# The value products of two attention units in one order, and two groups of small transfers issued by GpSimd instead of SyncE

## The chip, the cores and the metric

The kernel runs on one core of a Trainium2 chip. The core has five instruction queues: TensorE (PE, the matmuls, with its weight loads listed as PEld), VectorE (DVE), ScalarE (ACT), GpSimd (POOL) and SyncE (SP). SP issues almost all transfers (DMA); the 16 DMA engines of the core carry them out. The metric is device microseconds of one execution. Of the kernel before, three runs were timed, median 411.48 us (410.52 to 412.81); one more execution was profiled, which took 412.56 us with a span of 410.4 us between its first and last instruction, so 2.2 us lie outside the span.

## The reference

One decoder layer on 512 tokens of width 1024, in float32: two mixers read the same projection, and their outputs are merged and projected.

```
h = x @ w_in + b_in                      # q_a, kv_a, g_nsa, z_a, q_b, f_b, i_b, z_b, gm_a, gm_b
# mixer A: sparse attention, 8 heads in 2 groups, head size 64
o_cmp = softmax(q . kc) @ vc             # kc, vc: keys and values of compressed blocks
o_slc = softmax(q_rope . k_slc) @ v_slc  # blocks chosen; with 512 tokens all 8 blocks are
o_win = softmax(q_rope . k_win) @ v_win  # sliding window of 512
o_a   = g0 * o_cmp + g1 * o_slc + g2 * o_win      # gates: sigmoid(g_nsa), per head
# mixer B: gated linear recurrence in chunks of 64, 4 heads of 128
o_b   = hgrn2(q_b, f_b, i_b)
o_b   = o_b * rsqrt(mean(o_b ** 2) + eps) * norm_g
# merge
y = sigmoid(gm_a) * ((o_a * silu(z_a)) @ w_a) + sigmoid(gm_b) * ((o_b * silu(z_b)) @ w_b)
out = layer_norm(alpha * x + y @ w_out)
```

## The kernel before

**Projections.** Each large product is made of three float32r products (reduced-precision passes over float32 data): the weights and the activations are both split into a high and a low part, and hi·xh, hi·xl and lo·xh are added in PSUM. The weights of the projection come as a stream of tiles of 128 x 1024 (`wraw`, two buffers, one SP transfer each, issued three tiles ahead). For each tile ACT casts the high part (`whi`, L274), DVE subtracts to get the low part (`wlo`, L277; three buffers each), and `proj()` issues 24 products on PE, into one of two `pa` PSUM banks. Weight tile 25 is called `gb1` in the text that follows.

**The order of the work.** `proj()` calls `weave.tick()` once per two k-tiles (six products). Everything else is written as Python generators, started on `_Weave`; each `yield n` says after how many ticks the generator goes on, and the numbers come from the table `D`. So `D` decides where, between the projection's products, each other piece of work is recorded. PE's instructions and the transfers of each issuing queue run in exactly the recorded order (`keep_in_program_order`, in `T.matmul` and in `dma` at L150 and L151). The instructions of DVE and ACT are placed by a scheduler that reads the recorded program, so their order moves when the recorded order moves. Every queue is in order: an instruction that waits holds up all that stand behind it.

**Attention.** The 512 queries are four blocks i of 128; a block attends i + 1 key tiles of 128 in each of two branches (selected, window). The work is in six units, u0 to u5, which are (block 3, branch 0), (3, 1), (2, 0), (2, 1), (1, both), (0, both). `attn_scores` makes the scores in PSUM (`pss`, `pst`, `pso`, two banks each). DVE adds masks (L738), ACT exponentiates (L755), DVE or ACT scales by gate and denominator (L763, L766, L772, L774), and DVE transposes 32 x 32 blocks into the one `big` buffer (L788 to L791). Sixteen SP transfers of 32 rows (L802, shown by the profile with the line of `dma`, L151) then turn `big` into a `turn` buffer, of which there are two.

**The values.** When both units of a block are turned, `values(u)` (L808) multiplies the probabilities by the values: products of 64 x 64 on a quarter of the PE array each. `half` selects the rows 0 to 63 or 64 to 127 of the array, `ab` the columns; each half has a PSUM bank `pso` of its own. For block 3 there are eight tiles, four from each unit. Half 0 goes through the tiles 0 to 7, half 1 begins with tile i + 1, so with the second unit's tiles, and comes to the first unit's afterwards. Each product shows in the trace as two records.

**Mixer B's norm.** `hgrn_norm` transposes and sums the squared outputs of four heads (L512, L513), moves the partial sums between partitions by 16 small transfers (L518), adds them (L521, L522), takes the inverse root on ACT (L525, L526), spreads the result (L533, L534) and multiplies it in (L540, L541). `gates` computes the gates of the attention and moves those of the compressed branch, `gq`, into `gc` by 16 small transfers (L621); `cmp_probs` reads them at L691. Both groups are issued by SP, in the same queue as the weight tiles and the `turn` transfers. POOL only clears a few tiles and makes four small copies (L385).

Of the kernel before, what the change touches and what calls it, by code (L numbers as in the profile page):

```python
# [49 lines left out]
def _columns(name):  # L50

    c = np.arange(_COLS[name], _COLS[name] + 128)
    if name[0] == "q" and name[1] != "b" or name[:2] == "za":
# [16 lines left out]
D = dict(h0=6, h2=6, h3=14, h4=0, h5=7, h6=9, n0=20, n1=4, n2=4, n3=1, n4=3, c0=3, c1=5, c2=2, c3=0, r0=5, p0=2,  # L70
         p1=28, p2=0, s0=7, s2=15, s3=4, e0=4, e1=2, t0=6, t1=11, t2=6, t3=3, a4=8, a5=6, y=2, w0=2, w1=2, x0=0,
         x1=0, e2=2, e3=2, g=3, o0=0, o1=9, o2=9, v=10)
D.update({"x0.za0": 4, "o0.0": 6, "w0.35": 0, "y.o.3": 6, "o1.1": 3, "h2.0": 4, "y.m.6": 8, "w0.33": 5, "w1.10": 4,
# [62 lines left out]
def layer_kernel(ctx: ExitStack, tc: tile.TileContext, xT, xn, w0, wi, wf, wv, small, brow, consts,  # L136
# [13 lines left out]
    def dma(o, i):  # L150
        tc.keep_in_program_order(nc.sync.dma_start(o, i))  # L151
# [37 lines left out]
    def dma_act(o, i):  # L189
        tc.keep_in_program_order(A.dma_start(o, i))  # L190

# [312 lines left out]
    def hgrn_norm():  # L504
# [11 lines left out]
        for a in range(4):  # L516
            for b in range(4):
                dma(parts4[32 * a:32 * a + 32, 64 * b:64 * b + 64], part[32 * b:32 * b + 32])  # L518
            yield 1
# [87 lines left out]
    def gates():  # L607
# [11 lines left out]
        for a in range(4):  # L619
            for m in range(4):  # L620
                dma(gc[32 * m:32 * m + 32, a], gq[32 * a:32 * a + 32, m])  # L621
            yield 2
# [185 lines left out]
    def values(u):  # L808
# [4 lines left out]
        for n in range(len(tiles)):  # L813
            for half in range(2):
                v, st = tiles[(n + half * (i + 1)) % len(tiles)]
                br, j = units[v][1][st // (i + 1)], st % (i + 1)
                late = 2 * (j == i and half != br)
                for ab in range(2):
                    rows, c = slice(64 * half, 64 * half + 64), (128, NV)[br] * br + 64 * ab
                    T.matmul(accs[half][64 * ab:64 * ab + 64, 128 * late:512], vts[j][rows, c:c + 64],  # L820
                             probs[v][rows, st, late:4, 128 * ab:128 * ab + 128],
                             start=n == 0, stop=n == len(tiles) - 1)
# [383 lines left out]
```

## Time and profile before

| | us |
|---|---|
| median of three runs (lowest, highest) | 411.48 (410.52, 412.81) |
| profiled execution | 412.56 |
| its span | 410.4 |
| PE busy in the span | 402.4 (98%) |
| PE weight loads | 325.0 (79%) |
| DVE busy | 294.0 (72%) |
| ACT busy | 213.7 (52%) |
| POOL busy | 5.2 (1%) |

Times in rows of the profile are microseconds from the start of the span. A timeline row gives the start, the duration of a run of equal instructions, the engine, the line, the operation with output and inputs, and in brackets the idle time before it with what ended it. `SPq` is SP's queue as it issues transfers; such a row lasts as long as the issuing did, and the data land later. In the transfers' rows `turn<-big` are the sixteen transfers of a unit, `t<-t` at 32 x 64 the partial sums of mixer B, `gc<-gq` the gates and `wraw` the weight tiles. Engines overlap, so busy shares do not add up. The granted TensorE clock is 1.00 where nothing throttles it.

### The profile page before, as it was taken

What the parts mean: (1) busy time and instruction counts of PE and PEld (TensorE: products, weight loads), DVE (VectorE), ACT (ScalarE), POOL (GpSimd) and SP (SyncE); (2) the same over time, 40 slices, a digit from 0 to 9 for tenths busy, and PEclk for the clock granted to TensorE, in tenths of its full rate; (3) what the DMA queues carried; (4) which work ended last, traced back from release to release, by engine and by line L of the source; (5) the groups of instructions that cost most, each with busy time, mean ns of one, the idle gap of its engine ahead of it and who ended that gap; (6) DMA issues with size and microseconds to landing.
All of it is one profiled execution on the core that took longest, in us unless ns stands there. A gap on an engine that the chain in (4) does not pass through costs nothing.

```text
span 410.4 us, 6085 instructions
## 1 busy us (share of the span) xinstructions
PE 402.4 (98%) x2119; PEld 325.0 (79%) x2119; DVE 294.0 (72%) x675; ACT 213.7 (52%) x442; POOL 5.2 (1%) x17
## 2 busy tenths in 40 slices
PE   9999999999999999999998999999999999999994
PEld 8888888899888887778873878885867888888884
DVE  5906599787665888899999586866432879882773
ACT  3445461643225645786785596981223758458211
POOL 2000000001100000000000000000000000000000
PEclk9999999999999999999998999999999999999999
DMA  7975820143332423471184364364938861053121
GB/s 257 381 237 205 290 79 0 36 150 90 113 94 84 136 79 128 114 196 55 60 212 151 102 176 133 105 204 110 243 99 268 256 198 59 0 168 140 41 112 51
DMA packets 27182, 57.60 MB, mean 140 GB/s; under 512 B 5905, under 2 KB 8337, under 8 KB 27153
## 3 DMA queue, kind: packets, MB, share of 16 engines
q1 hardware_dynamic: 26720, 56.84, 44.5%
q10 hardware_dynamic: 432, 0.39, 0.3%
q8 instruction: 16, 0.26, 0.3%
q14 instruction: 14, 0.11, 0.1%
HBM read 42.12 MB, written 2.10 MB: 108 GB/s over the span
## 4 chain that ended last, share of the span: by engine, by line
PE 84%; DVE 7%; SPq 4%; DMA 2%; issue 1%; ACT 1%; DVEq 0%; ACTq 0%
PE pa L144 53%; PE pss L144 14%; PE pso L144 13%; PE pst L144 4%; SPq L151 4%; DVE t L738 2%; DVE wlo L277 1%; DMA turn<-big 1%; DVE big L788 1%; DVE t L512 1%; DVE t L513 1%; DMA t<-t 0%; ACT t L755 0%; PE pst L148 0%; DVE t L695 0%
## 5 line engine op out<-in xcount | busy, mean ns | idle before, releaser
L144 PE MATMUL pa<-t,whi 128*128 128x512 f32 x640 | 199.8, 393 | 0.0
L144 PEld LDWEIGHTS pa<-t,whi 128*128 128x128 f32 x640 | 118.3, 188 | 29.1 <-issue 4.4
L144 PE MATMUL pa<-t,wlo 128*128 128x512 f32 x320 | 124.7, 390 | 0.0
L277 DVE TENSOR_TENSOR wlo<-wraw,whi 128x1024 fp32r<-128x1024 f32 x44 | 53.6, 1217 | 52.2 <-ACT whi L274 48.8
L274 ACT CAST whi<-wraw 128x1024 fp32r<-128x1024 f32 x44 | 45.9, 1045 | 59.7 <-PE pa L144 50.4
L144 PEld LDWEIGHTS pa<-t,wlo 128*128 128x128 f32 x320 | 60.1, 188 | 12.8
L755 ACT ACTIVATE t<-t,sm_mn 128x512 f32<-128x512 f32 (+3 forms) x64 | 35.2, 553 | 13.3 <-DVE sm_mn L738 13.2
L144 PE MATMUL pso<-t,t 128*128 128x512 f32 (+2 forms) x158 | 33.2, 349 | 0.1
L144 PE MATMUL pss<-t,t 128*128 128x512 f32 (+2 forms) x158 | 30.2, 324 | 0.0
L144 PEld LDWEIGHTS pso<-t,t 128*128 128x128 f32 x158 | 25.8, 198 | 3.9 <-ACT t L233 0.4
L144 PE MATMUL pa<-t,t 128*128 128x512 f32 (+1 forms) x104 | 27.2, 367 | 0.0
L144 PEld LDWEIGHTS pss<-t,t 128*128 128x128 f32 x158 | 23.8, 190 | 2.8
L788 DVE STREAM_TRANSPOSE big<-t 128x512 f32<-128x512 f32 (+3 forms) x48 | 23.4, 523 | 0.4 <-PE pss L144 0.4
L144 PEld LDWEIGHTS pa<-t,t 128*128 128x128 f32 x104 | 18.4, 188 | 3.1
L774 ACT ACTIVATE t<-t,sm_mn 128x128 f32<-128x128 f32 (+3 forms) x39 | 18.0, 522 | 5.0 <-DVE sm_mn L766 4.9
L144 PE MATMUL pso<-turn,t 64*64 64x512 f32 (+1 forms) x160 | 19.1, 599 | 1.4 <-DMA turn<-big 1.4
L144 PE MATMUL pa<-turn,t 128*128 128x512 f32 x64 | 19.9, 389 | 0.0
L144 PE MATMUL pss<-t,whi 128*128 128x512 f32 x64 | 19.7, 389 | 0.0
L201 ACT CAST t<-t 128x512 fp32r<-128x512 f32 x16 | 9.6, 619 | 19.0 <-DVE t L1017 9.8
L144 PEld LDWEIGHTS pso<-turn,t 64*64 64x64 f32 x160 | 6.9, 142 | 13.2 <-issue 11.0
L144 PE MATMUL pst<-t,t 128*128 128x512 f32 (+2 forms) x80 | 15.1, 345 | 0.0
L999 ACT ACTIVATE t<-pa,hbias 128x512 f32<-128x512 f32 x16 | 10.9, 680 | 8.1 <-PE pa L144 8.1
(201 smaller groups left out, 520.9 us busy)
## 6 DMA issues: line engine op xcount, KB each, us to landing
wraw<-in_wf_dram SPq DMA_DIRECT2D x38, 512.0 KB, 3.5
turn<-big SPq DMA_DIRECT2D x48, 128.0 KB, 3.2
wraw<-in_wbr_dram SPq DMA_DIRECT2D x8, 512.0 KB, 4.2
t<-in_wout_dram SPq DMA_DIRECT2D x16, 256.0 KB, 4.5
turn<-big SPq DMA_DIRECT2D x32, 96.0 KB, 2.2
t<-in_wi_dram SPq DMA_DIRECT2D x8, 256.0 KB, 4.8
big<-in_w_dram SPq DMA_DIRECT2D x8, 256.0 KB, 6.4
t<-t SPq DMA_DIRECT2D x32, 64.0 KB, 2.0
```

Of the source, the lines that this page charges most:

```text
L144: return tc.keep_in_program_order(nc.tensor.matmul(*a, **k))
L151: tc.keep_in_program_order(nc.sync.dma_start(o, i))
L201: A.copy(dst_hi, src)
L274: A.copy(hi, raws[i])
L277: V.tensor_tensor(lo, raws[i], hi.bitcast(F32), ALU.subtract)
L512: V.transpose(sqT, osq[h][1])
L513: V.tensor_reduce(part[:, 16 * h:16 * h + 16], sqT.rearrange("p (c d) -> p c d", d=32), AX.X, ALU.add)
L738: V.tensor_tensor_reduce(out=p[:, c], in0=pg[ab][:, 256 * z:][:, c], in1=amask[:, 512 - n:512], op0=ALU.add, op1=ALU.min, scale=-0.125, sc ...
L755: A.activation(p, p, AF.Exp, bias=mn[:, h:h + 1], scale=-1.0, accum_out=den[:, h:h + 1])
L774: A.mul(p, p, d)
L788: V.transpose(to, of)
L999: A.activation(gm[name], ps, AF.Tanh, bias=hbias[:, m:m + 1], scale=0.5)
```

## The change

Three things are changed. First, `values(u)`: for the blocks i of 1 and more both halves go through the first unit's tiles and then the second's. The products are sorted by the columns that their half has done so far; a tile on the diagonal of the other half's branch has 256 columns and not 512, so that the halves come out of step by half a tile. For block 0 half 1 takes the tiles in reverse order, as before. Second, a function `dma_pool` issues transfers from POOL, and the 16 partial-sum transfers of `hgrn_norm` and the 16 transfers of `gates` use it. Third, the table `D` has other delays. Lines move by 1 behind the table, by 4 behind `dma_pool` and by 8 behind `values`: L277 is L281, L521 is L525, L738 is L742, L919 is L927.

```diff
-D = dict(h0=6, h2=6, h3=14, h4=0, h5=7, h6=9, n0=20, n1=4, n2=4, n3=1, n4=3, c0=3, c1=5, c2=2, c3=0, r0=5, p0=2,
+D = dict(h0=6, h2=6, h3=14, h4=0, h5=7, h6=9, n0=20, n1=4, n2=4, n3=0, n4=3, c0=4, c1=5, c2=4, c3=0, r0=5, p0=2,
...
+
+    def dma_pool(o, i):
+        tc.keep_in_program_order(G.dma_start(o, i))
...
         for a in range(4):
             for b in range(4):
-                dma(parts4[32 * a:32 * a + 32, 64 * b:64 * b + 64], part[32 * b:32 * b + 32])
+                dma_pool(parts4[32 * a:32 * a + 32, 64 * b:64 * b + 64], part[32 * b:32 * b + 32])
...
         for a in range(4):
             for m in range(4):
-                dma(gc[32 * m:32 * m + 32, a], gq[32 * a:32 * a + 32, m])
+                dma_pool(gc[32 * m:32 * m + 32, a], gq[32 * a:32 * a + 32, m])
...
         accs = PO(), PO()
-        for n in range(len(tiles)):
-            for half in range(2):
-                v, st = tiles[(n + half * (i + 1)) % len(tiles)]
+        todo = []
+        for half in range(2):
+            at = 0
+            for n, (v, st) in enumerate(tiles if i else tiles[::1 - 2 * half]):
                 br, j = units[v][1][st // (i + 1)], st % (i + 1)
                 late = 2 * (j == i and half != br)
-                for ab in range(2):
-                    rows, c = slice(64 * half, 64 * half + 64), (128, NV)[br] * br + 64 * ab
-                    T.matmul(accs[half][64 * ab:64 * ab + 64, 128 * late:512], vts[j][rows, c:c + 64],
-                             probs[v][rows, st, late:4, 128 * ab:128 * ab + 128],
-                             start=n == 0, stop=n == len(tiles) - 1)
+                todo.append((at, n, half, v, st, br, j, late))
+                at += 4 - late
+        for at, n, half, v, st, br, j, late in sorted(todo):
+            for ab in range(2):
+                rows, c = slice(64 * half, 64 * half + 64), (128, NV)[br] * br + 64 * ab
+                T.matmul(accs[half][64 * ab:64 * ab + 64, 128 * late:512], vts[j][rows, c:c + 64],
+                         probs[v][rows, st, late:4, 128 * ab:128 * ab + 128],
+                         start=n == 0, stop=n == len(tiles) - 1)
```

SP's queue around the transfers of units 0 to 3. Here `turn<-big` of 32 x 1024 are units 0 and 1, of 32 x 768 units 2 and 3; `t_1870` holds the partial sums. Before:

```order
L151 DMA turn<-big 32x1024 x16
L151 DMA wraw<-in_wf_dram 128x1024 x2
L151 DMA t_1870<-t_1870 32x64 x8
L151 DMA wraw<-in_wf_dram 128x1024
L151 DMA t_1870<-t_1870 32x64 x8
L151 DMA wraw<-in_wf_dram 128x1024
L151 DMA turn<-big 32x1024 x16
L151 DMA wraw<-in_wf_dram 128x1024 x5
L151 DMA turn<-big 32x768 x16
L151 DMA wraw<-in_wf_dram 128x1024 x3
L151 DMA turn<-big 32x768 x16
```

And now:

```order
L152 DMA turn<-big 32x1024 x16
L152 DMA wraw<-in_wf_dram 128x1024 x3
L152 DMA turn<-big 32x1024 x16
L152 DMA wraw<-in_wf_dram 128x1024 x6
L152 DMA turn<-big 32x768 x16
L152 DMA wraw<-in_wf_dram 128x1024 x2
L152 DMA turn<-big 32x768 x16
```

The partial sums are gone from between the transfers of units 0 and 1, one weight load has moved behind unit 1's, and one of the three between units 2 and 3 has moved out. On POOL the 16 gate transfers stand behind the four copies of L385 and ahead of two memsets, and the 16 partial-sum transfers are its last work.

PE's queue in the value products of block 3, with buffer numbers: `pso_2294` is half 0's bank and `pso_2295` half 1's; `t2_` are the values. Before (`turn_1874` is unit 0's buffer, `turn_2107` unit 1's):

```order
L144 MATMUL pso_2294<-turn_1874,t2_1019 64x512 x2
L144 MATMUL pso_2295<-turn_2107,t2_1019 64x512 x2
L144 MATMUL pso_2294<-turn_1874,t2_1038 64x512 x2
L144 MATMUL pso_2295<-turn_2107,t2_1038 64x512 x2
L144 MATMUL pso_2294<-turn_1874,t2_1071 64x512 x2
L144 MATMUL pso_2295<-turn_2107,t2_1071 64x512 x2
L144 MATMUL pso_2294<-turn_1874,t2_1137 64x512 x2
L144 MATMUL pso_2295<-turn_2107,t2_1137 64x512 x2
```

And now (`turn_1807` is unit 0's, `turn_2091` unit 1's):

```order
L145 MATMUL pso_2294<-turn_1807,t2_1019 64x512 x2
L145 MATMUL pso_2295<-turn_1807,t2_1019 64x512 x2
L145 MATMUL pso_2294<-turn_1807,t2_1040 64x512 x2
L145 MATMUL pso_2295<-turn_1807,t2_1040 64x512 x2
L145 MATMUL pso_2294<-turn_1807,t2_1071 64x512 x2
L145 MATMUL pso_2295<-turn_1807,t2_1071 64x512 x2
L145 MATMUL pso_2294<-turn_1807,t2_1139 64x512 x2
L145 MATMUL pso_2295<-turn_1807,t2_1139 64x256 x2
L145 MATMUL pso_2295<-turn_2091,t2_1019 64x512 x2
```

The block stands at the same place between the projection's products as before; within it the second unit's buffer is now first touched by the ninth pair of products and not by the second. The block of units 2 and 3 has moved 12 products earlier, that of unit 5 to a later place.

DVE's queue around the eight transposes of units 1 and 2's probabilities (L788 before, L792 now). Before, the subtract of weight tile 25 stood among the masks that read the scores:

```order
L738 ISA t_2225,sm_mn<-pss,t_321 128x384
L738 ISA sm_mn 128x1
L277 TENSOR_TENSOR wlo<-wraw,whi 128x1024
L738 ISA t_2227,sm_mn<-pst,t_321 128x384
L738 ISA sm_mn 128x1
L738 ISA t_2229,sm_mn<-pst,t_321 128x384
```

Now it stands behind the transposes, together with that of tile 26:

```order
L792 STREAM_TRANSPOSE big<-t_2063 128x3x4x32
L792 STREAM_TRANSPOSE big<-t_2065 128x3x4x32
L792 STREAM_TRANSPOSE big<-t_2067 128x3x4x32
L792 STREAM_TRANSPOSE big<-t_2069 128x3x4x32
L281 TENSOR_TENSOR wlo<-wraw,whi 128x1024 x2
L836 TENSOR_TENSOR asum<-asum,pso 128x4x4x32
```

Before, one subtract stood between these transposes and the sum into `asum` (L828, now L836). The cast of tile 25 on ACT (L274, now L278) has likewise moved to the place just ahead of that of tile 26. The sum of the partial sums (L521, now L525) stands earlier than before: one transpose of L699 and the subtract of tile 24 are ahead of it behind the transposes of unit 1, and a transpose, the L927 and a small product come between it and the spreading copies.

More of the change, by code (lines that the diff above doesn't have):

```diff
@@ L67 @@
     0, 128, 256, 260, 772, 1284, 1796, 2308, 2820)
-D = dict(h0=6, h2=6, h3=14, h4=0, h5=7, h6=9, n0=20, n1=4, n2=4, n3=1, n4=3, c0=3, c1=5, c2=2, c3=0, r0=5, p0=2,
-         p1=28, p2=0, s0=7, s2=15, s3=4, e0=4, e1=2, t0=6, t1=11, t2=6, t3=3, a4=8, a5=6, y=2, w0=2, w1=2, x0=0,
-         x1=0, e2=2, e3=2, g=3, o0=0, o1=9, o2=9, v=10)
-D.update({"x0.za0": 4, "o0.0": 6, "w0.35": 0, "y.o.3": 6, "o1.1": 3, "h2.0": 4, "y.m.6": 8, "w0.33": 5, "w1.10": 4,
[23 rows of a table removed]
+D = dict(h0=6, h2=6, h3=14, h4=0, h5=7, h6=9, n0=20, n1=4, n2=4, n3=0, n4=3, c0=4, c1=5, c2=4, c3=0, r0=5, p0=2,
+         p1=35, p2=1, s0=8, s2=18, s3=4, e0=4, e1=2, t0=6, t1=10, t2=6, t3=3, a4=14, a5=7, y=2, w0=2, w1=1, x0=0,
+         x1=0, e2=2, e3=2, g=3, o0=0, o1=9, o2=0, v=10)
+D.update({"o0.0": 6, "w0.35": 0, "y.o.3": 6, "o1.1": 3, "h2.0": 4, "y.m.6": 8, "w0.33": 5, "w1.10": 4, "y.m.0": 1,
[24 rows of a table added]
 def wait_of(step, *at):
```

45 rows, old and new, of the table x1 are left out of this document.

## The prediction

> **What bounds the kernel now.** I read the profiled execution's totals first, then what TensorE (PE) waits for, then PE's timeline around that wait.
>
> ```profile
> span 410.4 us, 6085 instructions
> PE 402.4 (98%) x2119; PEld 325.0 (79%) x2119; DVE 294.0 (72%) x675; ACT 213.7 (52%) x442; POOL 5.2 (1%) x17
> ...
> PE pso L144 <- DMA turn<-big: 1.4, 1, 1.4
> ```
>
> PE fills 98% of the span, so a transfer, a subtract or a cast matters only where PE stands still or runs slowly for it. In the middle of the kernel PE waits once for transfers: the value products of units 0 and 1, whose probabilities arrive in `turn` (the last row: microseconds in total, times, longest).
>
> ```profile
> 215.10 1.08 PE L144 MATMUL pso<-turn,t 64*64 64x512 f32 x4
> 217.55 8.35 PE L144 MATMUL pso<-turn,t 64*64 64x512 f32 x60 [1.37 <-DMA turn<-big]
> 225.84 0.50 PE L144 MATMUL pa<-t,whi 128*128 128x512 f32 x1
> ...
> 278.32 4.88 PE pso L144 x48
> ...
> 215.00:218.00 3.00, 1.63 (x9) 0.43 (x12) 2.99 (x12) 2.55 (x7) 0.00 (x0) 0.99 0.87 195
> 218.00:221.40 3.40, 3.40 (x20) 1.29 (x16) 3.40 (x8) 3.40 (x7) 0.00 (x0) 0.50 0.80 311
> 221.40:224.80 3.40, 3.40 (x38) 1.46 (x32) 3.40 (x8) 0.47 (x1) 0.00 (x0) 1.00 0.02 5
> ```
>
> The first three rows are PE's timeline (start, length): four records, a stop, the other sixty. The fourth, from the chain of waits, is the same kind of block for units 2 and 3. The window rows give length, busy time of PE, weight load, DVE, ACT and POOL with their instructions, the granted clock, DMA share and GB/s. From 218.0 to 221.4 the clock is 0.50 and PE does 20 records; in the next window of equal length it does 38 at 1.00.
>
> What the block loses: it takes 225.84 − 215.10 = 10.74 us. The later block has 48 records, 8 of half width, so 44 full ones in 4.88 us. This one has 64, 8 of half width, so 60 full ones: 4.88 × 60/44 = 6.65 us undisturbed. The loss is 10.74 − 6.65 = 4.1 us: 217.55 − 215.10 = 2.45 between start and second start, less the four records already done, and 3.4 us at half clock, worth 1.7.
>
> Why the tiles are late:
>
> ```profile
> 181.28 9.77 SPq L151 DMA_DIRECT2D wraw<-in_wf_dram  x2
> ...
> 199.25 0.33 SPq L151 DMA_DIRECT2D wraw<-in_wf_dram  x1
> 199.62 5.83 SPq L151 DMA_DIRECT2D t<-t  x8
> 205.57 0.50 SPq L151 DMA_DIRECT2D wraw<-in_wf_dram  x1
> 206.12 10.41 SPq L151 DMA_DIRECT2D turn<-big  x16
> ...
> 201.91 0.67 DVE L788 STREAM_TRANSPOSE big<-t 128x512 f32<-128x512 f32 x1
> ```
>
> Unit 1's last transpose ends at 202.6, but SP issues the second eight partial-sum transfers (5.83 us) and a weight load before it issues `turn` from 206.1 to 216.5. Unit 1's tiles therefore land until after 217, and half 1 before the change begins with just those tiles.
>
> **The change, part by part.** *Values in one order, and SP freed.* SP now goes from the third weight load straight to unit 1's `turn` transfers. They begin when the transposes allow, 202.6; at 10.41/16 = 0.65 us each the last is issued by 213.0 and, with the same gap that the old one shows (issued by 216.5, PE released at 217.55), the data are there by about 214.1, before the block starts at 215.1. Even a delay is covered: unit 0's tiles come first in both halves, 30 full records of 0.11 us, so unit 1 is needed only about 3 us into the block. The idle 1.37 us goes, and I take it that the half clock, which follows that stop and is not there in the later block, goes with it. Gain: **4.1 us**. Its lower end is 2.0 (stop and ramp gone, half clock kept: 4.1 − 1.7, less 0.4 for the records that overlap), should the clock drop for the density of the block rather than for the stop.
>
> *Sixteen partial-sum transfers on GpSimd (POOL).* No row shows a POOL transfer. The work that waits is L521 on DVE, which sums what they bring.
>
> ```profile
> 188.47 0.68 DVE L513 TENSOR_REDUCE t<-t 128x16 f32<-128x512 f32 x1
> 203.61 1.29 DVE L695 STREAM_TRANSPOSE t<-t 128x512 f32<-128x512 f32 x2
> 206.38 1.22 DVE L277 TENSOR_TENSOR wlo<-wraw,whi 128x1024 fp32r<-128x1024 f32 x1
> 207.52 0.60 DVE L521 TENSOR_REDUCE t<-t 128x64 f32<-128x256 f32 x1
> 208.96 1.43 DVE L533 COPY t<-t 128x512 f32<-128x512 f32 x4 [0.61 <-ACT t L526]
> ...
> 132.14 0.13 POOL L555 MEMSET t<- 128x16 f32 x1 [26.01 <-DVE t L203]
> ...
> t<-t SPq DMA_DIRECT2D x16, 8.0 KB, 2.1
> ```
>
> The sums are complete at 189.2. With a POOL pitch of c per transfer, the last issue ends at 189.2 + 16c, and its data land some 1.5 later (2.1 from issue to landing on SP, last row, less an issue of 0.6). In the new order one L695 transpose (0.65) and a subtract (1.22) stand between 203.6 and L521, so its turn comes at about 205.4. DVE then waits W = 189.2 + 16c + 1.5 − 205.4 = 16c − 14.7. Bounds of c: 0.13, a POOL memset, and 2.1, each transfer landed before the next. I take the nearest row, the same kind of transfer on SP, 5.83/8 = 0.73 at most and 0.65 for `turn`: **W = 0**, and it stays 0 up to c = 0.92. At 2.1 W is 18.9.
>
> The Trainium skill (DMA: Bandwidth & Descriptors, Specifications) puts the first byte of a GpSimd transfer at about 1 us, against about 0.6 for a queue like SP's. Read as a pitch, which no run here shows, that would make W an estimated 1.3 us, the rival of a new wait below.
>
> *A subtract moved behind eight transposes.* The subtract of weight tile 25 (gb1) leaves its place among the masks, and its cast goes to ACT's later pair.
>
> ```profile
> 211.90 1.23 DVE L277 TENSOR_TENSOR wlo<-wraw,whi 128x1024 fp32r<-128x1024 f32 x1
> ...
> 215.31 0.56 DVE L738 CUSTOM_DVE_ANT_0 t<-pso,t 128x384 f32<-128x384 f32 x1
> 222.39 3.79 DVE L788 STREAM_TRANSPOSE big<-t 128x384 f32<-128x384 f32 x8
> 226.10 1.19 DVE L277 TENSOR_TENSOR wlo<-wraw,whi 128x1024 fp32r<-128x1024 f32 x1
> ...
> 210.83 1.04 ACT L274 CAST whi<-wraw 128x1024 fp32r<-128x1024 f32 x1
> 220.84 1.03 ACT L274 CAST whi<-wraw 128x1024 fp32r<-128x1024 f32 x1
> ...
> 229.16 0.39 PE L144 MATMUL pa<-t,wlo 128*128 128x512 f32 x1
> ```
>
> Until now it ran at 211.90, 16 us ahead of PE's first use at 229.16. Now it follows the transposes, where a subtract stands at 226.10. That place comes 1.23 earlier, because its own row is gone from in front, and some 0.4 earlier because the new order puts L919 and L766 into the 0.61 that DVE waited for ACT at L533: about 224.5, so it ends at 225.7 + W. PE reaches its first use at 229.16 − 4.1 = 225.05. A new wait of **0.6 us + W** follows; PE has the `hi` products of that k-tile done and nothing else may pass. The cast, now the first of the pair at 220.84, ends near 221.9 and does not decide. Behind the subtract stands tile 26's, needed a whole tile (24 products) later, and the sum at L828.
>
> *W on its other path.* The masks of L738 free the second `pso` bank at 215.87; without the moved subtract, and with L521 earlier, at about 213.2 + W. For W above 1.9 PE waits there first, but what it waits there it does not wait at the subtract: the total stays 0.6 + W.
>
> *The gates' 16 transfers on POOL, and the later blocks.* `gc` is read at 186.5, near 80 us after the first of these issues, and the first instruction queued behind them on POOL, the memset at 132.14, is reached in time for any c below (132.1 − 107.8)/16 = 1.5; only above that would the compressed keys' sums behind the memset be late, by up to 16 × 2.1 − 24.3 = 9.3 at 2.1. On SP PE waited for nothing then. Cost 0.
>
> ```profile
> 107.75 2.44 SPq L151 DMA_DIRECT2D gc<-gq  x4
> 186.51 0.19 DVE L691 TENSOR_TENSOR sm_mx<-sm_mx,gc 128x16 f32<-128x16 f32 x1
> ...
> 259.66 1.04 DVE L788 STREAM_TRANSPOSE big<-t 128x384 f32<-128x384 f32 x2
> ...
> 262.25 10.07 SPq L151 DMA_DIRECT2D turn<-big  x16
> ```
>
> The block of units 2 and 3 stands 12 products (2.7 us) earlier in PE's order, and 3.5 earlier in time: 272.1 in place of 278.3, unit 3's tiles needed from 274.6. SP has one load fewer ahead of them, so `turn` starts at the transposes' end, 260.7, and has landed by 260.7 + 10.1 + 1.5 = 272.3. Margin 2.3 us: cost 0.
>
> **Sum.** −4.1 + 0.6 + 0 = −3.5 us on the profiled execution, whose time is 412.56 and span 410.4: 409.06, span 406.9. The runs shown have a median of 411.48, 1.08 lower; 3.5 off that is 408.0. Since half of this difference may be the very half clock, which other executions may not have, I forecast the middle, **408.5**.
>
> **Rivals.** *A new wait takes a part (POOL at about 1 us a transfer).* W = 1.3 at c = 1.0, the wait at the subtract is 1.9 and the gain 2.2: 412.56 − 2.2 = 410.4, or 412.1 if that stop brings back a half clock of 1.7. For it: an engine run by software has no row at SP's pitch. Against: the transfers are small and POOL has nothing else to do.
>
> *Slower: POOL is held off while DVE works.*
>
> ```profile
> 190.00:200.00 10.00, 10.00 (x55) 8.08 (x54) 8.96 (x21) 6.47 (x14) 0.00 (x0) 1.00 0.18 59
> ...
> 99.41 0.20 POOL L385 COPY gat<-t 128x24 f32<-128x24 f32 x1 [2.01 <-DVE t L381]
> 104.99 1.13 POOL L385 COPY gat<-t 128x24 f32<-128x24 f32 x1 [5.38 <-DVE t L381]
> ```
>
> DVE is busy 8.96 of 10 us just where POOL must issue. If POOL advances only in the gaps, it has about 1.7 us by 205.4, two to three transfers of 0.65; then DVE stands at L521 and lets the other 13 through: 13 × 0.65 + 1.5 gives W = 10.0, so 412.56 − 3.5 + 10.0 = 419.1. It decides from W = 3.5, c = 1.14, where the gain is gone. For it: the same small copy took POOL 0.20 us once and 1.13 another time. Against: even that is 0.9 us more, not the length of a DVE-busy stretch. The Trainium skill (SBUF — State Buffer, "DVE blocks DMA") states that such a lock stops GpSimd from writing descriptors, 620 ns becoming 3100, though for copies in a two-port mode; in this stretch few DVE rows are copies, and the trace can't show it.
>
> *The half clock is not the stop's.* Then 2.0 − 0.6 = 1.4 is left: 412.56 − 1.4 = 411.2, or 410.1 against the median. The records speak against it: the same products run at full rate in the later block.
>
> **How the numbers follow.** Forecast 0.54, new wait 0.20, held-off POOL 0.13, half clock kept 0.13. Half a percent of 411.48 is 2.06, about what can be told from no change: faster is below 409.42, slower above 413.54. Faster: nearly all of the forecast (0.49), a quarter of the new wait (0.05), a little of the last (0.02) = 0.56. Slower: held-off POOL and 0.03 from the new wait with the clock down = 0.16. The rest, 0.28, is the same. The range runs from the lowest run less 3.5 (407.0) to the new wait with the half clock (412.1), widened a little for run-to-run spread: 406.8 to 412.8.
>
> **What would show it.** Right: PE's timeline has one unbroken value block of about 6.7 us, no window at 0.50, a short PE wait for `wlo` L281 right behind it, POOL's transfers issued by about 200, and no DVE wait at L525. A DVE wait at L525 for a DMA gives W directly, and a long one proves the forecast wrong; so would a PE wait at `pso` for DVE's masks, or unit 3's block waiting for `turn`.

## The result, and the profile after

The changed kernel takes 409.05 us (median of 9 runs, 408.49 to 409.61) against 411.48 us before (9 runs, 410.44 to 412.98): a ratio of 0.994, 95% interval 0.9922 to 0.9958. The forecast was 408.5. The profiled execution took 409.05 us, 3.51 less than that of before. Its span, PE's waits and PE's timeline around the value block of units 0 and 1:

```profile
span 407.3 us, 6081 instructions
PE 399.8 (98%) x2119; PEld 323.8 (80%) x2119; DVE 293.6 (72%) x672; ACT 214.6 (53%) x445; POOL 20.8 (5%) x49
...
PE pso L145 <- PEq L1202: 0.8, 1, 0.8
...
214.89 6.67 PE L145 MATMUL pso<-turn,t 64*64 64x512 f32 x64
221.49 0.74 PE L145 MATMUL pa<-t,whi 128*128 128x512 f32 x2
225.10 0.50 PE L145 MATMUL pa<-t,wlo 128*128 128x512 f32 x1
397.47 3.28 PE L145 MATMUL pst<-t,t 128*128 128x256 f32 x26
...
218.00:221.40 3.40, 3.40 (x38) 1.18 (x30) 3.37 (x7) 3.40 (x7) 0.00 (x0) 1.00 0.04 13
```

All 64 records of the block are one row of 6.67 us; PE's one listed wait is the one at the program's start. In the window where the clock was 0.50 it is 1.00, with 38 records instead of 20. The work behind the block ends with these rows, first of before, then of the change (PE's last products, and DVE's last instruction):

```profile
401.40 3.28 PE L144 MATMUL pst<-t,t 128*128 128x256 f32 x26
405.82 1.54 DVE L1125 SCALAR_TENSOR_TENSOR big<-big,sm_ss,t 128x512 f32<-128x512 f32 x3
```

```profile
401.89 1.54 DVE L1133 SCALAR_TENSOR_TENSOR big<-big,sm_ss,t 128x512 f32<-128x512 f32 x3
```

So the difference of the two executions can be read in pieces:

| piece | before | change | difference |
|---|---|---|---|
| start of the span to start of the block | 215.10 | 214.89 | −0.2 |
| start of the block to the next `pa` product | 225.84 − 215.10 = 10.74 | 221.49 − 214.89 = 6.60 | −4.1 |
| from there to PE's last products | 401.40 − 225.84 = 175.56 | 397.47 − 221.49 = 175.98 | +0.4 |
| from there to DVE's end | 407.36 − 401.40 = 5.96 | 403.43 − 397.47 = 5.96 | 0 |
| DVE's end to the end of the span | 410.4 − 407.36 = 3.0 | 407.3 − 403.43 = 3.9 | +0.8 |
| time outside the span | 412.56 − 410.4 = 2.2 | 409.05 − 407.3 = 1.8 | −0.4 |

The third piece is a new wait for the subtract of tile 25 (from the `pa` product behind the block to the one behind the subtract's first use, PE takes 225.43 − 221.49 = 3.94 us, and took 229.38 − 225.84 = 3.54 before), the fifth a longer end of the program that the prediction did not have. The first piece is not the change's: the same stretch varied by as much between two executions of one kernel (215.10 and 214.98 before, 214.89 and 214.81 after). What the queues did in the profile after, SP and POOL with their issues, then transfers of POOL (KB each, median us to landing), then DVE:

```profile
181.83 17.48 SPq L152 DMA_DIRECT2D wraw<-in_wf_dram  x3
202.33 11.38 SPq L152 DMA_DIRECT2D turn<-big  x16
...
189.21 7.99 POOL L194 DMA_DIRECT2D t<-t  x16 [52.70 <-DVE t L517]
...
t<-t POOLq DMA_DIRECT2D x16, 8.0 KB, 1.6
...
203.95 1.19 DVE L281 TENSOR_TENSOR wlo<-wraw,whi 128x1024 fp32r<-128x1024 f32 x1
205.06 0.61 DVE L525 TENSOR_REDUCE t<-t 128x64 f32<-128x256 f32 x1
220.15 3.79 DVE L792 STREAM_TRANSPOSE big<-t 128x384 f32<-128x384 f32 x8
223.86 2.32 DVE L281 TENSOR_TENSOR wlo<-wraw,whi 128x1024 fp32r<-128x1024 f32 x2
```

POOL issues at a pitch of 7.99/16 = 0.50 us; by the trace the last sum lands at 198.25, 6.8 us before L525, which waits for nothing. Unit 1's transfers begin at 202.33, as soon as its transposes are done, and the last of them lands at 215.57. The subtract of tile 25 is the first of the two at 223.86 and ends at about 225.0; PE's product on it starts at 225.10.

### The profile page after: what moved, and what is told of

Its sections match the earlier page's. It is cut to its first block, busy times and chain, and to the rows that moved or that the text cites. A ratio compares the mean times of both kernels' runs of the same rounds, so it can differ in the third digit from the quotient of the medians.

```text
span 407.3 us, 6081 instructions
## 1 busy us (share of the span) xinstructions
PE 399.8 (98%) x2119; PEld 323.8 (80%) x2119; DVE 293.6 (72%) x672; ACT 214.6 (53%) x445; POOL 20.8 (5%) x49
## 3 DMA queue, kind: packets, MB, share of 16 engines
q0 software_dynamic: 1024, 0.15, 0.2%
## 4 chain that ended last, share of the span: by engine, by line
PE 90%; DVE 7%; issue 1%; DVEq 0%; ACT 0%; ACTq 0%
PE pa L145 60%; PE pss L145 15%; PE pso L145 11%; PE pst L145 4%; DVE big L792 2%; DVE wlo L281 1%; DVE t L742 1%; DVE t L538 1%; DVE t L544 1%; DVE t L545 0%; PE pst L149 0%; DVE t L537 0%; DVE t L927 0%; DVE big L1133 0%; DVE t L776 0%
## 5 line engine op out<-in xcount | busy, mean ns | idle before, releaser
L281 DVE TENSOR_TENSOR wlo<-wraw,whi 128x1024 fp32r<-128x1024 f32 x44 | 53.5, 1217 | 35.1 <-ACT whi L278 35.1
L278 ACT CAST whi<-wraw 128x1024 fp32r<-128x1024 f32 x44 | 45.7, 1046 | 53.5 <-PE pa L145 35.5
L145 PEld LDWEIGHTS pa<-t,wlo 128*128 128x128 f32 x320 | 60.1, 188 | 13.3 <-DVE wlo L281 0.5
L792 DVE STREAM_TRANSPOSE big<-t 128x512 f32<-128x512 f32 (+3 forms) x48 | 23.5, 523 | 2.2 <-PE pss L145 2.2
L145 PE MATMUL pso<-turn,t 64*64 64x512 f32 (+1 forms) x160 | 16.4, 552 | 0.0
L742 DVE CUSTOM_DVE_ANT_0 t<-pss,t 128x128 f32<-128x128 f32 (+3 forms) x24 | 10.2, 476 | 7.4 <-PE pss L145 7.4
```

Source lines behind the costliest of these rows:

```text
L145: return tc.keep_in_program_order(nc.tensor.matmul(*a, **k))
L278: A.copy(hi, raws[i])
L281: V.tensor_tensor(lo, raws[i], hi.bitcast(F32), ALU.subtract)
L742: V.tensor_tensor_reduce(out=p[:, c], in0=pg[ab][:, 256 * z:][:, c], in1=amask[:, 512 - n:512], op0=ALU.add, op1=ALU.min, scale=-0.125, sc ...
L792: V.transpose(to, of)
```

## The experiments

The theory: the block loses 4.1 us because its second product meets tiles that land too late, and the half clock follows from that stop. Its rivals: the clock belongs to the dense products; the gain needs GpSimd's issue; the gain needs both parts. "Median span" is over the runs of a kernel.

**Order of the values alone.** The kernel before with the new loop of `values` (the last hunk of the diff) and nothing else.

> Only the order of the value products is the new one; the delays and SyncE's queue are those of before, with the partial sums ahead of unit 1's transfers. Theory (a product on late data is the whole cause): unit 1's transfers still land from 217.3 to about 218.6, but are needed only at 215.1 + 3.0 = 218.1, so a stop of at most 0.5 us stays and no half clock: block 6.7 to 7.2 us instead of 10.74, time 3.5 to 4.1 below before, about 407.7 against a median of 411.5. Rival (the half clock belongs to the dense block, not to the stop): a window at 0.50 stays, block about 8.4 us, time about 409.5. Rival (the freed queue is what counts): no more than 1 us gained.

Measured 409.0 us (8 runs, ratio 0.9934, 0.9907 to 0.9961), median span 406.95. SP's issue, the block, a window in it, and then PE's weight loads for half 1 and the mask on DVE that they wait for:

```profile
205.75 10.26 SPq L151 DMA_DIRECT2D turn<-big  x16
...
214.69 7.48 PE L144 MATMUL pso<-turn,t 64*64 64x512 f32 x64
...
218.00:221.40 3.40, 3.40 (x34) 1.91 (x32) 3.40 (x7) 2.88 (x6) 0.00 (x0) 1.00 0.78 266
...
215.51 0.23 PEld L144 LDWEIGHTS pso<-turn,t 64*64 64x64 f32 x8 [0.63 <-DVE sm_mn L738]
...
214.89 0.56 DVE L738 CUSTOM_DVE_ANT_0 t<-pso,t 128x384 f32<-128x384 f32 x1
```

The transfers are as late as before, and the block takes 7.48 us in place of 10.74, at full clock, with no transfer moved to GpSimd: 0.3 above its forecast of 6.7 to 7.2. The time is 1.3 above its forecast of 407.7. The 0.8 us that the block has more than the change is lost in both halves, for different reasons. Half 1 begins 0.82 us after half 0 (0.02 in the change), because the mask L738 still reads its `pso` bank until 215.45 (last two rows). Half 0 reaches unit 1's tiles at 218.2 and goes on at 218.87, when the last of their transfers has landed at 218.74. The halves run side by side on the array, so these two do not add up; that either alone would leave some 0.7 is an estimate from these starts.

**Transfers on GpSimd alone.** The kernel before with `dma_pool` for both groups; values in the old order.

> Only the two groups of transfers go to GpSimd; the order of the value products and the delays are those of before, so half 1 still begins with unit 1. Theory (late data): unit 1's transfers begin at about 202.6 or behind one weight load more, and land by 214 to 215.5, before or just as the block starts at 215.1: stop under 0.5 us, no half clock, block about 6.7 us; the end of the program is 0.8 us longer as in the change: 411.5 - 4.1 + 0.8 = 408.2. Rival (the order of the halves is what counts, or clock follows density): block over 8 us and a window at 0.50, time 410 or more.

Measured 409.76 us (11 runs, ratio 0.9947, 0.9927 to 0.9968), median span 407.9.

```profile
204.00 10.88 SPq L151 DMA_DIRECT2D turn<-big  x16
...
215.12 7.19 PE L144 MATMUL pso<-turn,t 64*64 64x512 f32 x64
```

The old order, with tiles that land 2 us earlier, has no half clock and a block of 7.19. The sums' earlier arrival also moves the masks of L738: half 1's bank is free at 213.68. What is left is half 1's wait for unit 1's tiles, 0.54 us (it starts at 215.66, behind a transfer that lands at 215.42). So either part removes the stop; the two are not added to one another. The time is 1.5 us above the forecast of 408.2: 0.5 of it is the block, and the rest fits a median of before that holds less of the half clock than its profiled execution (below).

**The change with both groups back on SyncE.**

```diff
-                dma_pool(parts4[32 * a:32 * a + 32, 64 * b:64 * b + 64], part[32 * b:32 * b + 32])
+                dma(parts4[32 * a:32 * a + 32, 64 * b:64 * b + 64], part[32 * b:32 * b + 32])
...
-                dma_pool(gc[32 * m:32 * m + 32, a], gq[32 * a:32 * a + 32, m])
+                dma(gc[32 * m:32 * m + 32, a], gq[32 * a:32 * a + 32, m])
```

> The change with its new delays and its order of the values, but both groups of small transfers are issued by SyncE again. Theory (the order of the values alone covers the late tiles, and the longer end is GpSimd's queue): the block keeps its 6.7 us or at most 0.5 more, the end of the program is as short as before (3.0 us behind the last transfer's issue and not 3.9), so the time is 0.4 to 0.8 below the change: about 408.4. Rival (GpSimd's issue is needed for the gain): a stop of over 1 us and a half clock in the block, time 411 or more.

Measured 409.43 us (10 runs, ratio 0.9931, 0.9905 to 0.9956), median span 407.6, not below the change but 0.35 above it.

```profile
215.38 6.67 PE L145 MATMUL pso<-turn,t 64*64 64x512 f32 x64
226.61 0.50 PE L145 MATMUL pa<-t,wlo 128*128 128x512 f32 x1 [1.12 <-DVE wlo L281]
...
403.40 1.54 DVE L1133 SCALAR_TENSOR_TENSOR big<-big,sm_ss,t 128x512 f32<-128x512 f32 x3
```

The block keeps its 6.67 us and the end of the program is short again (408.0 − 404.94 = 3.1), as the theory had it. The miss is mainly the wait for the subtract of tile 25: 1.12 us by its row, 0.10 in the change. DVE sums the partial results later when SP brings them, and the subtract behind it moves with it. The block also starts 0.5 us later than in the change (215.38), but in this execution PE was 0.6 us later from its first products on (8.29 and 7.69). With the new delays GpSimd's issue is worth that wait, and costs the longer end.

**The changed kernel again, on the same chip as these three.**

> The changed kernel itself, for the comparison on one chip: ratio to before 0.994, block 6.7 us, clock 1.00 throughout the block, end of the program 3.9 us behind the last issue, in this execution too.

Measured 409.05 us (8 runs, ratio 0.9926, 0.9899 to 0.9953), median span 407.25: block 6.67 at full clock, 3.8 us at the end. As expected.

**Partial sums on ScalarE's queue.** The first experiment's kernel with this edit:

```diff
-                dma(parts4[32 * a:32 * a + 32, 64 * b:64 * b + 64], part[32 * b:32 * b + 32])
+                dma_act(parts4[32 * a:32 * a + 32, 64 * b:64 * b + 64], part[32 * b:32 * b + 32])
```

> New order of the value products, delays of before, gates' transfers on SyncE, and the 16 partial-sum transfers issued by ScalarE's queue, which transfers at the start and end use already; GpSimd issues none. If ScalarE has room for 16 issues of 0.35 to 0.6 us between its casts, this has the block at 6.7 us, no wait for the subtract of tile 25 and the short end of the program: span 407.3 - 0.4 - 0.8 = 406.1, time about 408.0, better than the change. Rival (ScalarE's casts come late: twelve issues, some 7 us, stand between two casts): TensorE waits 1 to 6 us for casts or subtracts, time 409 to 414.

Measured 410.65 us (12 runs, ratio 0.9953, 0.9934 to 0.9971): the rival. ACT's issues, its next cast, and PE's two waits:

```profile
197.13 6.87 ACTq L190 DMA_DIRECT2D t<-t  x9
204.04 1.06 ACT L274 CAST whi<-wraw 128x1024 fp32r<-128x1024 f32 x1 [6.19 <-DMA t<-t]
...
206.31 0.72 PE L144 MATMUL pa<-t,whi 128*128 128x512 f32 x2 [1.10 <-ACT t L921]
217.65 4.58 PE L144 MATMUL pso<-turn,t 64*64 64x512 f32 x40 [0.87 <-DVE sm_mn L738]
```

ScalarE, which has work of its own, stands still while its queue issues, 6.19 us here, and PE waits for what comes behind. The block takes 7.13 us and not the 6.7 of the forecast, again with a mask of L738 that frees half 1's bank late.

**Twice the work for GpSimd.** The change with 16 more transfers ahead of the partial sums:

```diff
+        for a in range(4):
+            for b in range(4):
+                dma_pool(spare[32 * a:32 * a + 32, 64 * b:64 * b + 64], part[32 * b:32 * b + 32])
         for a in range(4):
             for b in range(4):
```

> The change with 16 more transfers of the same size and source, to a spare tile, issued by GpSimd ahead of the partial sums. Theory (pitch 0.50 us, landing 1.6 us after its issue starts, VectorE in order): the last sum lands at 189.2 + 32 x 0.5 + 1.1 = 206.3, VectorE waits W = 1.2 us at L525 from 205.06 on, the subtract of tile 25 ends 1.2 later, TensorE's wait there grows from 0.4 to 1.6: time 409.05 + 1.2 = 410.3. Rival (the subtract has other cover, or VectorE makes the time up): unchanged 409.0. Rival (GpSimd is slowed by VectorE when it issues for longer): W of 3 us or more.

Measured 409.69 us (8 runs, ratio 0.9943, 0.9914 to 0.9972), median span 407.9, 0.65 above the change.

```profile
196.69 7.94 POOL L194 DMA_DIRECT2D t<-t  x16
...
206.85 0.62 DVE L530 TENSOR_REDUCE t<-t 128x64 f32<-128x256 f32 x1 [1.26 <-DMA t<-t]
...
204.92 0.73 PE L145 MATMUL pa<-t,whi 128*128 128x512 f32 x2 [0.46 <-ACT t L930]
226.15 0.50 PE L145 MATMUL pa<-t,wlo 128*128 128x512 f32 x1 [0.72 <-DVE wlo L281]
```

W is 1.26 us where 1.2 was forecast; that it fits so well is partly luck, since the last sum landed 0.4 later than reckoned (206.73) and DVE came to L530 0.5 later (205.59). PE pays it in two places: 0.46 for a `pa` bank that ACT frees later, and 0.72 at the subtract of tile 25. The time is 0.6 below the forecast of 410.3; in the profile the end of the program is 3.4 us, 0.4 shorter than the change's. POOL's pitch stays 0.50 through 16 us in which DVE is nearly always busy (15.51 us of the 16.7 from 188.0 to 204.7).

**One transfer on GpSimd.** The kernel before with a single gate transfer moved:

```diff
-                dma(gc[32 * m:32 * m + 32, a], gq[32 * a:32 * a + 32, m])
+                (dma_pool if a == m == 0 else dma)(gc[32 * m:32 * m + 32, a], gq[32 * a:32 * a + 32, m])
```

> The kernel before with a single one of the gates' 16 transfers on GpSimd. It is to split the longer end of the program (3.05 us from the start of the last output transfer's issue to the end before, 3.9 with 32 transfers on GpSimd). If the end pays per semaphore (eight more waits of 0.06) and a fixed part for GpSimd's queue (0.4): about 3.4 to 3.5. If all of it is fixed: 3.9. If all of it is per semaphore: 3.1. The value block stays as before, near 10 us.

One execution: 413.07 us, span 410.9. Its block is like before's, with a stop of 2.49 us and 3.41 us at half clock.

```profile
406.41 1.54 DVE L1128 SCALAR_TENSOR_TENSOR big<-big,sm_ss,t 128x512 f32<-128x512 f32 x3
```

The end is 410.9 − 407.95 = 2.9 us, no longer than the 3.0 of before; from the last issue it is the case "all per semaphore". Over all profiles the end is 2.9 to 3.1 us in the executions with no or one transfer on GpSimd, and 3.4 to 4.0 in the five with 32 or 48 (the doubled work 3.4, the change 3.8 twice, GpSimd alone and the both-parts kernel below 4.0). So the price belongs to the many transfers and not to the queue's first use. Part of it can be seen in the records of the queues: after the last output has landed, SP passes eight waits in the change and four in the kernel before, 0.06 us each. The rest, up to 0.4 us on POOL in four of the five, is not explained.

**A longer stop.** The kernel before, with four small transfers more ahead of unit 1's:

```diff
+                if v == 1:
+                    for k in range(4):
+                        dma(spare[32 * k:32 * k + 32], of[32 * k:32 * k + 32, 0, 0:64])
                 for a in range(4):
                     for b in range(4):
```

> The kernel before with four more small transfers (to a spare tile) on SyncE ahead of unit 1's, 2.5 us more, so that the stop in the value block grows from 2.45 to about 5 us. Theory (the stop itself makes the clock drop, by chance of where it falls in a period of about 3.4 us): the half clock is in every execution, mean granted clock 0.994 or below, time 411.4 + 2.5 and no group without the half clock, so 413.5 to 416. Rival (the drop comes from the dense products, or by chance of the execution and not from the stop): again two groups as in the kernel before, with and without it, about 413 and 415.

Measured 415.04 us (10 runs, ratio 1.0062, 1.0037 to 1.0087).

```profile
218.76 8.32 PE L144 MATMUL pso<-turn,t 64*64 64x512 f32 x60 [3.29 <-DVE t L534]
...
218.70:222.10 3.40, 3.34 (x16) 1.16 (x20) 3.40 (x6) 2.07 (x4) 0.00 (x0) 0.51 0.97 330
```

PE stands for 3.29 us, and the half clock is there. (The row names L534 of DVE; the last transfer that half 1 needs landed at 218.57.) All ten executions have a mean granted clock of 0.987 to 0.995. They are not one group: six have 0.993 to 0.995 and spans of 411.6 to 412.2, four 0.987 to 0.991 and 413.0 to 413.8. The profiled one is of the first six, so the faster group too has the half clock, as the theory had it; the next run suggests what parts the groups, a half clock of twice the length.

**The kernel before again.**

> The kernel before once more, for a second trace. If the half clock comes and goes with the execution (as the mean clocks of its runs, 0.994 and 0.998, say): either a block near 10 us with a window at 0.50 and a span near 410.7, or a block near 9 us at 1.00 throughout and a span near 408.6, with the same stop of about 2 us in both.

One execution: 415.43 us, span 412.8.

```profile
218.75 9.56 PE L144 MATMUL pso<-turn,t 64*64 64x512 f32 x60 [2.69 <-DVE t L540]
...
218.00:221.00 3.00, 2.25 (x12) 0.88 (x16) 3.00 (x7) 3.00 (x6) 0.00 (x0) 0.50 1.01 298
221.00:224.60 3.60, 3.60 (x20) 1.10 (x16) 3.60 (x8) 1.04 (x1) 0.00 (x0) 0.50 0.12 46
```

Neither of the two expected cases: SP issued unit 1's transfers at the same times as in the first profile (206.20 and 206.12), the last of them landed 0.9 us later and the fourteenth, the last one that half 1 needs, 1.2 later (218.50 and 217.31), and the stop was 2.69 us instead of 1.37. The row names L540 of DVE as what ended the wait; but in the first profile the same product ran at 217.55, ahead of that L540, so it does not wait for it, and the transfer is what came last. The half clock lasted 6.83 us by the trace, twice the 3.41 of the first profile. Together these make a block of 13.3 us. What the runs say without a trace: of 86 executions of the kernel before that were timed beside the experiments, 41 have a mean clock of 0.987 to 0.995 and spans of 410.2 to 412.8 (median 410.8), 45 have 0.996 to 0.999 and 408.2 to 409.6 (median 408.7), with nothing between. No trace of the second group was taken, so its block was not seen.

**Both parts with the old delays.** The kernel before with the new loop of `values` and `dma_pool` for both groups.

> Both parts of the change (the order of the value products and both groups of transfers on GpSimd), with the delays of before: the subtract of tile 25 keeps its early place, ahead of the masks. Theory (the wait of 0.4 us behind the block belongs to the new delays): block 6.7 us, no wait for that subtract, end of the program 3.8 us behind VectorE's last instruction as in the change: span 407.3 - 0.4 = 406.9, time about 408.6. Rival (the old delays cost it elsewhere): 409.0 or more.

Measured 409.14 us (8 runs, ratio 0.9937, 0.9916 to 0.9959), median span 407.0.

```profile
215.24 6.67 PE L144 MATMUL pso<-turn,t 64*64 64x512 f32 x64
```

The block is as in the change and PE waits for no subtract behind it; the median span is 0.25 lower, where 0.4 was forecast, and the time does not differ. The new delays bring nothing that these runs can tell.

**All partial sums in one burst on SyncE.** One line taken out, once with the new order of the values, once without:

```diff
                 dma(parts4[32 * a:32 * a + 32, 64 * b:64 * b + 64], part[32 * b:32 * b + 32])
-            yield 1
         yield D["n1"]
```

> The new order of the value products with the delays of before and nothing on GpSimd; one line is taken out, the pause of a tick after each four partial-sum transfers, so that SyncE issues all 16 in a row before the third weight load. Theory (the queue was late because a weight load that waits for its buffer stood between two groups of eight): the sums are issued from 191 to 201, unit 1's transfers begin at 202.6 as in the change, block 6.7 us, no wait for the subtract of tile 25, end of the program 3.1 us behind VectorE's last instruction: span 407.3 - 0.4 - 0.75 = 406.1, time about 408.0, 1 us under the change. Rival (the sums' reduction or a later subtract now waits): 409 or more.

> The kernel before with that one line taken out and nothing else. Theory (late data alone is the cause): unit 1's transfers land by about 214.5, before the block starts; block 6.7 to 7.1, no half clock in any execution, time 408.0 to 408.5: the whole gain of the change and more. Rival (half 1 starting with unit 1 leaves a stop): block of 8 us or more, some executions with a mean clock of 0.994, time 409.5 or more.

Both forecasts failed: 414.43 us (12 runs, ratio 1.0058, 1.0034 to 1.0082) and 415.74 us (9 runs, ratio 1.0078, 1.0052 to 1.0104). SP issued the sums in one row as expected, and unit 1's transfers from 203.79 and 204.24, some 1.4 us later than expected. The block takes 6.67 us in both; but it begins at 221.30 and 222.60, when the last tile has long landed (216.98 and 217.71), so these two runs say nothing on the order of the values. The loss is elsewhere, ten microseconds earlier; of the first kernel, PE, a window, and ACT:

```profile
209.30 0.82 PE L144 MATMUL pa<-t,whi 128*128 128x512 f32 x2 [4.59 <-ACT t L920]
...
209.20:212.60 3.40, 3.30 (x9) 2.59 (x10) 3.40 (x6) 2.52 (x4) 0.00 (x0) 0.59 0.90 216
...
204.67 2.14 ACT L773 ACTIVATE t<-t,sm_mn 128x384 f32<-128x384 f32 x4 [3.35 <-DVE sm_mn L765]
206.72 0.24 ACT L524 ACTIVATE t<-t 128x64 f32<-128x64 f32 x1
206.99 0.26 ACT L525 ACTIVATE t<-t 128x64 f32<-128x64 f32 x1
207.26 1.28 ACT L193 ACT_TABLE_LOAD   x1
208.56 0.69 ACT L920 ACTIVATE t<-pa,hbias 128x512 f32<-128x512 f32 x1
```

With the recorded place of the sums the scheduler also moved ACT: the scaling of unit 2, the root of the norm and a table load now stand ahead of L920, which frees a `pa` bank that PE needs at 204.7. PE stops for 4.59 us (4.58 in the second kernel), and every one of the 21 executions of the two kernels has a mean clock of 0.987 to 0.994. The expectation had reckoned with SP and DVE and left ACT out. Here the stop lies among ordinary projection products, and the clock drops all the same.

## Why the prediction was right

**The gain of the block** (4.1 us): measured 10.74 − 6.60 = 4.14, stop and half clock both gone. The cause holds, with one correction to the step "values in one order, and SP freed": its two parts do the same thing twice. The order alone gives a block of 7.48, the transfers alone 7.19, both 6.67 us. Of the 4.1 us, the second part to come, whichever it is, is worth 0.5 to 0.8. One reading in this step was wrong and did no harm: unit 1's data were to be there by 214.1, before the block. The last tile landed at 215.57, 0.7 us into it. The gap of 1 us that was carried over from the kernel before ran from the last issue to PE's release, but that release came with the transfer at 217.31, and two more landed up to 219.15. The new order is what covered it.

**The half clock goes with the stop.** By their mean clock, idle PE of 4.59 us brings it in 21 of 21 executions, 3.29 us (as profiled) in 10 of 10, a stop of 1.4 to 2.7 us (two profiles of before) in 41 of 86; the six traces with a stop of 1.37 us or more all show it, and the eight others, whose longest stop there is 1.12 us, have no half clock ahead of the end of the program. The kernels without it have one group of spans each: the order alone 406.7 to 407.3, GpSimd alone 407.3 to 408.5, the change 406.7 to 407.8, the others 0.9 to 1.5 wide but for one execution of the doubled kernel (409.8, the rest 407.4 to 408.1). The rival "the half clock is not the stop's" falls: it came to ordinary products too.

The clock records of the traces also tell why a short stop brings it only sometimes. In all fourteen the clock changes only at whole multiples of 3.413 us from the first record. In the middle of the program it drops after 59, 60, 62, 62, 63 and 63 such periods and stays down for one (3.41 us, four traces) or two (6.83 us, two traces). The first record lies 3.7 to 7.0 us into the span, differently in each execution, so the same stop falls differently into these periods. TensorE had been busy for 4 to 60% of the period ahead of each drop. After 67% or more the full clock stayed in the middle of the program, but in one trace it stayed after 51% too, and the half clock went on into a second period after 72% in one trace and 58% in the other; no sharp limit comes out of these traces. A trace of before without the half clock was not taken, so for the 45 executions this is what fits and not what was seen. The Trainium skill (TensorE: Matmul & The Clock Gate, Part 1) names a free-running activity window of about 3.4 us, after an idle one of which the clock halves. The traces agree with the length and the free running. That a stop of 1.37 us was enough here is more than the Trainium skill says there, and the measurement decides.

**W = 0, POOL near SP's pitch.** Right, and faster than the row that it was taken from: 0.50 instead of 0.65, landing 1.6 us after the issue instead of SP's 2.1. The doubled transfers gave W = 1.26 against 1.2 forecast. The rival "POOL is held off while DVE works" is out for this mix of DVE work: in the change DVE was busy for 6.95 of the 8.2 us in which POOL issued, in the doubled kernel for 15.51 of 16.7, and the pitch was the same. The lock of the Trainium skill (SBUF — State Buffer, "DVE blocks DMA") is for copies in a two-port mode, and this says nothing of those. The later first byte that the Trainium skill gives GpSimd's transfers (DMA: Bandwidth & Descriptors, Specifications) is not seen in the time from issue to landing of these small transfers.

**The subtract behind the transposes** (0.6 us): right in place, sized a little too high: 0.4 measured. DVE came to it at 223.86 and not at 224.5, PE to its first use 0.2 earlier than reckoned.

**What failed: the end of the program.** The step that moved transfers to POOL was priced only where they are issued and where their data are awaited, at zero. It costs 0.8 us behind the last output transfer, which no row of the kernel before could show, but which a bound should have held. That the sum of −3.5 met the measured −3.51 is luck: this +0.8 was cancelled by −0.2 ahead of the block, −0.4 outside the span and the −0.2 at the subtract.

**The later blocks.** The block of units 2 and 3 began at 271.60 (272.1 was forecast) and waited for nothing.

**What the median showed.** The forecast of 408.5 rested on half of the 1.08 us between the median and the profiled execution being the half clock. It was rightly suspected, and larger: the spans with and without it differ by 2.1 us. Against the group without it the change gains 408.7 − 407.3 = 1.4 us of span, against the other 3.5; the medians differ by 2.4 because before is split nearly in halves. The change also removes this spread (1.1 us over its nine runs, 2.5 before), which fits the same cause.

## What to carry to other kernels

When an in-order engine meets late data, look first whether work on data already there can go ahead of it: here sixteen products in another order gave all but 0.8 us of the block's 4.1, without the longer end of the program that moving 32 transfers to another queue brought (which gave all but 0.5). Price a stop of TensorE with the half clock that may follow it (here one or two periods of 3.41 us), and compare kernels with and without such a stop over many executions, since one profile shows only one of the cases. When a block is still too long after an edit, look at what each half of it waits for: here one was short of a PSUM bank and the other of data. After an edit to the recorded order read the new order of every engine, the ones that were not meant too: one line taken out cost 4.6 us on an engine that it does not name.

## What had not been expected

The same 8 KB transfers between partitions were issued and landed sooner from GpSimd (0.50 and 1.6 us) than from SyncE (0.6 to 0.7 and 2.1); the gates' 1 KB transfers landed alike (1.6 and 1.7). Thirty-two of them made the end of the program 0.3 to 0.9 us longer, one did not. The same issue times of SP gave landings 0.9 us apart in two executions of one kernel, which moved a stop from 1.4 to 2.7 us. The clock changed only on a grid of 3.413 us.
